# Second feed-forward matmul: six groups by seven products, low parts of the left operands on GpSimd

## The chip, the core and the metric

The kernel runs on one core of a Trainium2 chip. A core has TensorE (PE in the profile, with PEld for its weight loads), VectorE (DVE), ScalarE (ACT), GpSimd (POOL) and SyncE (SP, which issues the DMAs). Each has its own instruction stream, and they wait for each other by semaphores. The metric is the device time of one execution, in microseconds (us).

## What is computed

One layer of a streaming encoder: a modulated RMSNorm, a wide input projection, a gated branch and a matrix-memory branch, an output projection, and then the part that matters here, on 512 positions (`SEQ`) of width 1024:

```python
xn = modulate(rmsnorm(h, norm2_g[l]), sh2, sc2)
ff = jnp.square(jax.nn.relu(xn @ w_ff1[l])) @ w_ff2[l]
h = h + g2[:, None, :] * ff
```

and a final RMSNorm. `w_ff1` is 1024 x 4096 and `w_ff2` is 4096 x 1024, both in fp32.

## The kernel before

**Split operands.** Every fp32 operand of a matmul is split in two fp32r parts: a high part, rounded by a copy on ScalarE, and a low part, the operand minus the high part. A product is then three matmuls (`mm3`, lines 116 to 119): high by high, high by low, low by high. For the weights `w_pair` does this (ScalarE line 1082, VectorE line 1083; tiles `wh_g`/`wl_g` or `wh_x`/`wl_x`, 128 x 1024 elements). For the left operands, the activations, `hl` does it (ScalarE line 1099, VectorE line 1100; tiles `hsh`/`hsl`, 128 x 512 elements; the first two lie in `hs` tiles). The low parts for queries and keys early in the kernel are formed on GpSimd already (line 439), from operands of the same size as those of `hl`.

**Groups and products.** The second feed-forward matmul sums over 4096 rows of `w_ff2`. The first 3072 are taken in six groups of 512. In a group the activations form a 2 x 2 arrangement (`a11`, `a12`, `a21`, `a22`: two halves of the rows, two halves of the positions), and the weights too (`F11`, `F12`, `F21`, `F22`: two halves of the rows, two halves of the columns). A group marked "W" needs seven products of sums and differences of these (P1 to P7) instead of the plain eight. A group marked "S" takes the eight plainly, each added to the banks where it belongs (P2, P3, P4, E). Before, `GROUPS` is "WWWWWS". A "W" group needs in exchange: one difference of activations at the end of the first feed-forward matmul (`minus_a21`, line 1017), one of weights and three of activations in the first pass (lines 1115 and 1117 to 1119), and three of weights in the second pass (lines 1123, 1127, 1131), all on VectorE.

**Passes.** All groups are gone through twice. In the first pass a "W" group does P1, P2, P7, P3, in the second P5, P6, P4. `plan_` lists the steps, 43 of them, one per product and group. A step has 12 matmuls of 128 x 512 (two blocks of 128 positions, two blocks of 128 rows, three matmuls). Each product of the seven adds up over the groups in two PSUM banks of its own (`gP1` and so on). The banks are read on ScalarE or VectorE by `after` when a product's last step is past, and combined into `r` tiles.

**Order.** The loop over `plan_` asks for the operands of five steps ahead (`prefetch_step(5)`). Six high and six low tiles of activations (`hs_tile`) and five of weights are there, so a tile is written again when TensorE is done with a step before. A scheduler then orders each engine's stream. Weights come by DMAs from SyncE (`F` tiles, line 1060), seven in the air at most. Inside a group the differences of activations are made in place: lines 1117 to 1119 overwrite `a21`, `a12` and `a11` after `hl` has read them.

**Behind the passes.** The last 1024 rows of `w_ff2` are multiplied plainly, in pieces of 128 rows: four as they come (24 matmuls each), and four together at the end. Their banks are `ob`, for the first 256 positions, and, for the others, the two banks of P4 and the two of E, which go on with what the passes left there. The `r` tiles are meanwhile multiplied by the gate and added to the residual (`gated`, lines 1178 and 1179), and then the final norm follows.

Of the kernel before, what the change touches and what calls it, by code (L numbers as in the profile page):

```python
# [8 lines left out]
F32 = mybir.dt.float32  # L9
# [40 lines left out]
def block_kernel(ctx, tc, vecs_d, rows_d, ws_d, x_d, w_ada, w_in, w_out, w_ff1, w_ff2, out_d):  # L50
    nc = tc.nc
    act, dve, pool, pe, sp = nc.scalar, nc.vector, nc.gpsimd, nc.tensor, nc.sync
# [6 lines left out]
    def bank(nm):  # L59
        return psum.tile([P, 512], F32, tag="ps", name=nm)  # L60
# [55 lines left out]
    def mm3(out, ah, al, bh, bl, start, stop):  # L116
        pe.matmul(out, lhsT=ah, rhs=bh, start=start, stop=False)  # L117
        pe.matmul(out, lhsT=ah, rhs=bl, start=False, stop=False)  # L118
        pe.matmul(out, lhsT=al, rhs=bh, start=False, stop=stop)  # L119
# [488 lines left out]
    for i in range(TB):  # L608
        for j in range(i + 1):
            src = li[:, blk[i]] if j == i else frames[i][:, blk[j]]  # L610
# [114 lines left out]
    for half in range(2):  # L725
        cs = slice(half * 512, (half + 1) * 512)
# [7 lines left out]
    for half in range(2):  # L734
        cs = slice(half * 512, (half + 1) * 512)
# [23 lines left out]
    for half in range(2):  # L759
        cs = slice(half * 512, (half + 1) * 512)  # L760
# [6 lines left out]
        for k in range(4 * half, 4 * half + 4):  # L767
# [4 lines left out]
            h_, l_ = hl[:, 0], hl[:, 1]  # L772
# [237 lines left out]
        prefetch_op(2)  # L1010
        return bk.rearrange("p (f t) -> p f t", f=2)

    GROUPS = "WWWWWS"

    def minus_a21(n):
        if GROUPS[n:n + 1] == "W":
            dve.tensor_sub(out=hq[n, 0, 1], in0=hq[n, 0, 0], in1=hq[n, 0, 1])
# [21 lines left out]

    NF = len(GROUPS)  # L1040
    NK = FF // P
    KF = 4 * NF

    def later(kind, pas):
        return {("W", 0): ("P1", "P2", "P7", "P3"), ("W", 1): ("P5", "P6", "P4"),
                ("S", 0): ("P2", "P3", "P2", "P3"), ("S", 1): ("P4", "E", "P4", "E")}[kind, pas]
# [41 lines left out]
    def hs_tile(q):  # L1088
        return hsp.tile([P, 2, 256], F32R, tag="hs" + q, name=f"hs{q}{count[1]}", bufs=6)

    def hl(src):
        i = count[1]
        count[1] += 1
        if i < 2:
            both = fp.tile([P, 2, 2, 256], F32R, tag="sc", name=f"hs0{i}", bufs=2)
            h_, l_ = both[:, 0], both[:, 1]
        else:
            h_, l_ = hs_tile("h"), hs_tile("l")
        act.copy(out=h_, in_=src)  # L1099
        dve.tensor_sub(out=l_, in0=src, in1=h_.bitcast(F32))  # L1100
        return h_, l_

    def passes():
        for n in range(2):
            for nh in range(2):
                yield hl(hq[n, nh, 0]), w_pair(left.get(), left)
        for pas in range(2):
            for n, kind in enumerate(GROUPS):
                a11, a12, a21, a22 = hq[n, 0, 0], hq[n, 1, 0], hq[n, 0, 1], hq[n, 1, 1]
                if kind == "W" and pas == 0:  # L1110
                    if n > 1:
                        yield hl(a11), w_pair(left.get(), left)
                        yield hl(a12), w_pair(left.get(), left)
                    b12, b22 = right.get(), right.get()
                    dve.tensor_sub(out=b12, in0=b22, in1=b12)  # L1115
                    yield hl(a21), w_pair(b12, right)
                    dve.tensor_sub(out=a21, in0=a22, in1=a21)
                    dve.tensor_sub(out=a12, in0=a12, in1=a21)
                    dve.tensor_add(out=a11, in0=a21, in1=a11)
                    yield hl(a12), w_pair(b22, right)  # L1120
                elif kind == "W":
                    b11, b12 = left.get(), right.get()
                    dve.tensor_sub(out=b12, in0=b12, in1=b11)
                    left.more()
                    yield hl(a11), w_pair(b12)
                    b22 = right.get()
                    dve.tensor_sub(out=b22, in0=b22, in1=b12)  # L1127
                    right.more()
                    yield hl(a21), w_pair(b22)
                    b21 = left.get()  # L1130
                    dve.tensor_sub(out=b21, in0=b21, in1=b22)
                    right.more()
                    yield hl(a22), w_pair(b21, left)
                else:
                    for a_ in ((a11, a12), (a21, a22))[pas]:
                        x_ = hl(a_)
                        yield x_, w_pair(left.get(), left)
                        yield x_, w_pair(right.get(), right)

    plan_ = [(0, key) for key in ("P1", "P2") * 2 + ("P7", "P3") * 2]  # L1140
    plan_ += [(0, key) for kind in GROUPS[2:] for key in later(kind, 0)]
    plan_ += [(1, key) for kind in GROUPS for key in later(kind, 1)]
    gen = passes()
    ready = []

    def prefetch_step(m):
        while len(ready) < m:
            s_ = next(gen, None)
            if s_ is None:
                return  # L1150
            ready.append(s_)
# [13 lines left out]
    def hs_pair(kp):  # L1165
        for th in range(2):
            hsq[kp, th] = hl(hq[kp // 2, kp % 2, th])

    acc_b, res = {}, {}

    def rtile(nm, t):
        res[nm, t] = hsp.tile([P, 512], F32, name=f"r{nm}{t}")
        return res[nm, t]
# [7 lines left out]
    def after(key):  # L1181
        for t in range(2):
            b_ = acc_b.get((key, t))
            if key == "P1":
                act.copy(out=rtile("1", t), in_=b_)
            elif key == "P7":
                dve.tensor_add(out=rtile("7", t), in0=res["1", t], in1=b_)
            elif key == "P3":
                dve.tensor_add(out=rtile("3", t), in0=res["1", t], in1=b_)
            elif key == "P2":  # L1190
                dve.tensor_add(out=res["1", t], in0=res["1", t], in1=b_)
            elif key == "P6":
                dve.tensor_add(out=res["3", t], in0=res["3", t], in1=b_)
                dve.tensor_add(out=res["7", t], in0=res["7", t], in1=b_)
            elif key == "P5":
                dve.tensor_add(out=res["3", t], in0=res["3", t], in1=b_)
                dve.tensor_add(out=rtile("5", t), in0=res["7", t], in1=b_)

    last_of = {key: max(i for i, p_ in enumerate(plan_) if p_[1] == key) for _, key in plan_}
    end0 = max(i for i, p_ in enumerate(plan_) if p_[0] == 0)  # L1200
    jobs = {}
    for i_, keys in ((last_of["P7"] + 2, ("P1", "P7")), (end0 + 2, ("P3", "P2")),
                     (last_of["P4"] if GROUPS[-1] == "W" else last_of["P6"] + 3, ("P6", "P5"))):
        jobs.setdefault(i_, []).extend(keys)
    NS = len(plan_)
    for i, (pas, key) in enumerate(plan_):
        prefetch_step(5)
        (h_, l_), (wh, wl) = ready.pop(0)
        first = (key, 0) not in acc_b
        for t in range(2):  # L1210
            if first:
                acc_b[key, t] = bank(f"g{key}{t}")
            ts_ = slice(t * P, (t + 1) * P)
            for j in range(2):
                mm3(acc_b[key, t], h_[:, j, ts_], l_[:, j, ts_], wh[:, j], wl[:, j], first and j == 0,
                    i == last_of[key] and j == 1 and key not in ("P4", "E"))
        for key_ in jobs.get(i, ()):
            after(key_)
        if i == end0:
            sp.dma_start(out=fing, in_=rows_d[5].partition_broadcast(P))  # L1220
        if NS - i <= 4:
            ws_ff.prefetch(max(0, 4 - (NS - i)))
        if i == NS - 2:
            hs_pair(KF // 2)
# [1 line left out]
    ps_stack.close()  # L1226
    lwp = ff.enter_context(tc.tile_pool(name="lwp", bufs=1, side="right"))
    o_banks = [[bank(f"ob{t}{hf}") for hf in range(2)] for t in range(2)]
    o_banks += [[acc_b["P4", t], acc_b["E", t]] for t in range(2)]
    late = [(nm, t, row + t, hf) for nm, row, hf in (("1", 0, 0), ("3", 0, 1), ("7", 2, 0), ("5", 2, 1)) for t in range(2)]  # L1230

    def ff2_piece(k, last=False):
# [13 lines left out]
    def mm_f2(k, t, hf, wh, wl, stop):  # L1246
        cs = slice(hf * 512, (hf + 1) * 512)
        h_, l_ = (v[:, k % 2, (t % 2) * P:(t % 2 + 1) * P] for v in hsq[k // 2, t // 2])
        mm3(o_banks[t][hf], h_, l_, wh[:, 0, cs], wl[:, 0, cs], k == KF and t < 2, stop)

    for k in range(KF, NK - LAST):
        wh, wl = ff2_piece(k)
        for t in range(TB):
            for hf in range(2):
                mm_f2(k, t, hf, wh, wl, False)
        for _ in range(2):
            if late:
                gated(*late.pop(0))
# [46 lines left out]
    t = TB - 1  # L1305
# [72 lines left out]
```

## Time and profile before

| | us |
|---|---|
| median of 3 runs (806.1 to 807.3) | 807.0 |
| the profiled execution | 806.75 |
| its span in the trace | 805.0 |
| passes, first matmul to the first of the plain rows | 636.03 to 754.01 |

A row of instructions reads: start, duration, engine, line, operation, output and inputs by the program's names, and in brackets how long the engine was idle before and who ended that. A row of groups reads: count, total and mean duration in ns, and idle time before. The granted clock of TensorE is its share of full speed, 0.994 over the whole of this execution.

### The profile page before, as it was taken

What the parts mean: (1) busy time and instruction counts of PE and PEld (TensorE: products, weight loads), DVE (VectorE), ACT (ScalarE), POOL (GpSimd) and SP (SyncE); (2) the same over time, 40 slices, a digit from 0 to 9 for tenths busy, and PEclk for the clock granted to TensorE, in tenths of its full rate; (3) what the DMA queues carried; (4) which work ended last, traced back from release to release, by engine and by line L of the source; (5) the groups of instructions that cost most, each with busy time, mean ns of one, the idle gap of its engine ahead of it and who ended that gap; (6) DMA issues with size and microseconds to landing.
All of it is one profiled execution on the core that took longest, in us unless ns stands there. A gap on an engine that the chain in (4) does not pass through costs nothing.

```text
span 805.0 us, 11479 instructions
## 1 busy us (share of the span) xinstructions
PE 792.7 (98%) x4375; PEld 688.1 (85%) x4375; DVE 621.1 (77%) x938; ACT 404.2 (50%) x610; POOL 43.0 (5%) x62
## 2 busy tenths in 40 slices
PE   7999999999999999999999999999999999999996
PEld 6887888888988888888888899999999978888885
DVE  5889766774843348997847579888888799999966
ACT  5458566274533233242435247666666756646324
POOL 2004020121000000100000110000000000000000
PEclk8999999999999999999999999999999999999999
DMA  8974331143223388669337240333332466765302
GB/s 273 265 227 117 119 104 51 29 126 110 79 79 105 105 268 312 206 210 324 122 102 261 78 132 28 105 105 106 106 115 70 178 220 222 252 213 184 114 30 104
DMA packets 76423, 119.87 MB, mean 149 GB/s; under 512 B 5712, under 2 KB 38608, under 8 KB 76368
## 3 DMA queue, kind: packets, MB, share of 16 engines
q1 hardware_dynamic: 76368, 119.14, 46.6%
q8 instruction: 34, 0.56, 0.3%
q14 instruction: 21, 0.17, 0.1%
HBM read 117.02 MB, written 2.10 MB: 148 GB/s over the span
## 4 chain that ended last, share of the span: by engine, by line
PE 91%; DVE 2%; DMA 2%; ACT 2%; issue 1%; POOL 0%; SPq 0%; POOLq 0%; DVEq 0%
PE P L118 6%; PE P L117 6%; PE P L119 6%; PE gP L119 4%; PE gP L117 4%; PE gP L118 4%; PE qk L282 4%; PE wo L117 1%; PE wo L119 1%; PE wo L118 1%; PE cp L241 1%; PE k1b L117 1%; PE gb0b L118 1%; PE q1b L119 1%; PE gb0b L119 1%
## 5 line engine op out<-in xcount | busy, mean ns | idle before, releaser
L1099 ACT CAST hsh<-h 128x512 fp32r<-128x512 f32 x45 | 26.7, 620 | 26.9 <-PE gP L118 15.3
L1082 ACT CAST wh_g<-F 128x1024 fp32r<-128x1024 f32 x27 | 28.1, 1052 | 16.8 <-DVE F L1127 3.7
L119 PE MATMUL gP<-wh_g,hsl 128*128 128x512 f32 x92 | 35.8, 391 | 0.6 <-DVE hsl L1100 0.6
L118 PE MATMUL gP<-wl_g,hsh 128*128 128x512 f32 x92 | 35.8, 389 | 0.0
L117 PE MATMUL gP<-wh_g,hsh 128*128 128x512 f32 x92 | 35.7, 390 | 0.0
L1083 DVE TENSOR_TENSOR wl_g<-F,wh_g 128x1024 fp32r<-128x1024 f32 x27 | 32.9, 1225 | 0.8 <-ACT wh_g L1082 0.8
L921 ACT CAST wh_T<-T 128x1024 fp32r<-128x1024 f32 x21 | 22.0, 1048 | 20.0 <-PE P L118 18.4
L117 PE MATMUL P<-x2h,wh_B 128*128 128x256 f32 x112 | 31.6, 282 | 0.0
L118 PE MATMUL P<-x2l,wh_B 128*128 128x256 f32 x112 | 31.6, 282 | 0.0
L119 PE MATMUL P<-x2h,wl_B 128*128 128x256 f32 x112 | 31.6, 282 | 0.0
L921 ACT CAST wh_B<-B 128x1024 fp32r<-128x1024 f32 x21 | 22.0, 1049 | 16.4 <-PE P L118 15.4
L1100 DVE TENSOR_TENSOR hsl<-h,hsh 128x512 fp32r<-128x512 f32 x45 | 29.9, 692 | 0.3 <-ACT hsh L1099 0.3
L922 DVE TENSOR_TENSOR wl_T<-T,wh_T 128x1024 fp32r<-128x1024 f32 x21 | 25.7, 1224 | 3.0 <-ACT wh_T L921 2.9
L922 DVE TENSOR_TENSOR wl_B<-B,wh_B 128x1024 fp32r<-128x1024 f32 x21 | 25.6, 1220 | 0.0
L96 DVE TENSOR_TENSOR wl_gb<-raw_gb,wh_gb 128x1024 fp32r<-128x1024 f32 x8 | 9.8, 1224 | 19.7 <-ACT wh_gb L95 19.6
L118 PE MATMUL gP<-wl_x,hsh 128*128 128x512 f32 x64 | 24.9, 389 | 0.0
L117 PE MATMUL gP<-wh_x,hsh 128*128 128x512 f32 x64 | 24.9, 389 | 0.0
L119 PE MATMUL gP<-wh_x,hsl 128*128 128x512 f32 x64 | 24.9, 389 | 0.0
L667 DVE SCALAR_TENSOR_TENSOR accg<-arg,c_act,accg 128x1024 f32<-128x1024 f32 x14 | 18.0, 1283 | 6.5 <-DMA arg<-in_w_ada 6.3
L95 ACT CAST wh_ga<-raw_ga 128x1024 fp32r<-128x1024 f32 x8 | 8.4, 1052 | 27.2 <-PE ga0b L119 16.3
L976 ACT ACTIVATE h<-h 128x512 f32<-128x512 f32 x28 | 17.7, 632 | 8.5 <-DVE h L1036 4.0
L1082 ACT CAST wh_x<-F 128x1024 fp32r<-128x1024 f32 x16 | 16.6, 1050 | 9.5 <-DVE F L1115 3.9
(616 smaller groups left out, 2818.7 us busy)
## 6 DMA issues: line engine op xcount, KB each, us to landing
F<-in_w_ff SPq DMA_DIRECT2D x48, 512.0 KB, 4.2
B<-in_w_ff SPq DMA_DIRECT2D x28, 512.0 KB, 3.8
ar<-in_w_ada SPq DMA_DIRECT2D x64, 128.0 KB, 3.4
arg<-in_w_ada SPq DMA_DIRECT2D x16, 512.0 KB, 5.9
raw_f<-in_w_ff SPq DMA_DIRECT2D x12, 512.0 KB, 3.6
raw_o<-in_w_in SPq DMA_DIRECT2D x8, 512.0 KB, 4.1
raw_mv<-in_w_in SPq DMA_DIRECT2D x8, 512.0 KB, 3.6
raw_gb<-in_w_in SPq DMA_DIRECT2D x8, 512.0 KB, 3.7
```

Of the source, the lines that this page charges most:

```text
L117: pe.matmul(out, lhsT=ah, rhs=bh, start=start, stop=False)
L118: pe.matmul(out, lhsT=ah, rhs=bl, start=False, stop=False)
L119: pe.matmul(out, lhsT=al, rhs=bh, start=False, stop=stop)
L282: pe.matmul(bk, lhsT=wx[:, kk, f * P:(f + 1) * P], rhs=xx[k], start=k == 0 and ps_ == 0, stop=k == KT - 1 and ps_ == 2)
L667: dve.scalar_tensor_tensor(out=acc, in0=raw, scalar=c_act[:, k:k + 1], in1=acc, op0=ALU.mult, op1=ALU.add)
L921: act.copy(out=wh, in_=src)
L922: dve.tensor_sub(out=wl, in0=src, in1=wh.bitcast(F32))
L976: act.activation(dst, src, AF.Relu)
L1082: act.copy(out=wh, in_=src)
L1083: dve.tensor_sub(out=wl, in0=src, in1=wh.bitcast(F32))
L1099: act.copy(out=h_, in_=src)
L1100: dve.tensor_sub(out=l_, in0=src, in1=h_.bitcast(F32))
```

## The change

The last group becomes a "W" group as well, so that every group has seven products. The two banks of E are gone; the plain rows behind the passes get two fresh banks instead (`obr0`, `obr1`), so P6, which now goes to three results, is read into three `r` tiles, after P5 and at the end of the passes. And `hl` forms its low part on GpSimd instead of VectorE.

```diff
-    GROUPS = "WWWWWS"
+    GROUPS = "WWWWWW"
...
         act.copy(out=h_, in_=src)
-        dve.tensor_sub(out=l_, in0=src, in1=h_.bitcast(F32))
+        pool.tensor_sub(out=l_, in0=src, in1=h_.bitcast(F32))
...
-            elif key == "P6":
-                dve.tensor_add(out=res["3", t], in0=res["3", t], in1=b_)
-                dve.tensor_add(out=res["7", t], in0=res["7", t], in1=b_)
             elif key == "P5":
                 dve.tensor_add(out=res["3", t], in0=res["3", t], in1=b_)
                 dve.tensor_add(out=rtile("5", t), in0=res["7", t], in1=b_)
+            elif key == "P6":
+                for nm in ("3", "7", "5"):
+                    dve.tensor_add(out=res[nm, t], in0=res[nm, t], in1=b_)
...
-                     (last_of["P4"] if GROUPS[-1] == "W" else last_of["P6"] + 3, ("P6", "P5"))):
+                     (last_of["P5"] + 1, ("P5",)), (last_of["P6"] + 1, ("P6",))):
...
-    o_banks += [[acc_b["P4", t], acc_b["E", t]] for t in range(2)]
+    o_banks += [[acc_b["P4", t], bank(f"obr{t}")] for t in range(2)]
...
-        mm3(o_banks[t][hf], h_, l_, wh[:, 0, cs], wl[:, 0, cs], k == KF and t < 2, stop)
+        mm3(o_banks[t][hf], h_, l_, wh[:, 0, cs], wl[:, 0, cs], k == KF and (t < 2 or hf == 1), stop)
```

How this moves instructions shows at three places. On GpSimd, the stretch from the second norm (`rs2`) to the final one (`rs3`), which was empty; `h100` and its like are the activations, with the group as the first digit:

```order
 L76 TENSOR_TENSOR rs2_83<-rs2_83,mhalf_79 128x1
-L1284 TENSOR_TENSOR rs3_7460<-rs3_7460,mhalf_79 128x1 x4
+L1100 TENSOR_TENSOR hs00_6243<-h000_4528,hs00_6243 128x512
+L1100 TENSOR_TENSOR hs01_6252<-h010_4529,hs01_6252 128x512
+L1100 TENSOR_TENSOR hsl3_6279<-h100_4597,hsh3_6278 128x512
+L1100 TENSOR_TENSOR hsl4_6289<-h110_4599,hsh4_6288 128x512
+L1100 TENSOR_TENSOR hsl5_6300<-h001_4530,hsh5_6299 128x512
```

It now holds 50 such subtractions: 42 for the steps and 8 for the plain rows (before, VectorE had 39 and 8).

On VectorE, in the second pass at the fifth group (`F1243` is a weight tile of that group), before:

```order
L1123 TENSOR_TENSOR F1243_6944<-F1243_6944,F1143_6977 128x1024
L1100 TENSOR_TENSOR hsl35_7066<-h400_5311,hsh35_7065 128x512
L1127 TENSOR_TENSOR F2242_6967<-F2242_6967,F1243_6944 128x1024
L1083 TENSOR_TENSOR wl_g36_7070<-F1243_6944,wh_g36_7069 128x1024
L1100 TENSOR_TENSOR hsl36_7087<-h401_5312,hsh36_7086 128x512
L1083 TENSOR_TENSOR wl_g37_7091<-F2242_6967,wh_g37_7090 128x1024
L1131 TENSOR_TENSOR F2142_6992<-F2142_6992,F2242_6967 128x1024
L1100 TENSOR_TENSOR hsl37_7108<-h411_5314,hsh37_7107 128x512
```

and after, from the same difference on:

```order
L1123 TENSOR_TENSOR F1243_6957<-F1243_6957,F1143_6990 128x1024
L1083 TENSOR_TENSOR wl_x33_7012<-F1235_6866,wh_x33_7011 128x1024
L1127 TENSOR_TENSOR F2242_6980<-F2242_6980,F1243_6957 128x1024
L1083 TENSOR_TENSOR wl_x34_7035<-F2234_6899,wh_x34_7034 128x1024
L1131 TENSOR_TENSOR F2142_7005<-F2142_7005,F2242_6980 128x1024
L1178 TENSOR_TENSOR r10_6890<-r10_6890,rowg2_4096 128x512
L1083 TENSOR_TENSOR wl_g35_7058<-F2134_6932,wh_g35_7057 128x1024
L1123 TENSOR_TENSOR F1251_7028<-F1251_7028,F1151_7061 128x1024
L1083 TENSOR_TENSOR wl_g36_7083<-F1243_6957,wh_g36_7082 128x1024
```

The three subtractions of line 1100 have left VectorE's stream, and the differences of the sixth group (`F1251`) and a first instruction of `gated` have come in between the weight splits.

On VectorE, behind the last weight split of the passes, where P5 and P6 are read out of their banks, before:

```order
L1083 TENSOR_TENSOR wl_g42_7184<-F2250_7038,wh_g42_7183 128x1024
L1193 TENSOR_TENSOR r30_6912<-r30_6912,gP60_6898 128x512
L1194 TENSOR_TENSOR r70_6784<-r70_6784,gP60_6898 128x512
L1193 TENSOR_TENSOR r31_6914<-r31_6914,gP61_6905 128x512
L1194 TENSOR_TENSOR r71_6786<-r71_6786,gP61_6905 128x512
L1196 TENSOR_TENSOR r30_6912<-r30_6912,gP50_6871 128x512
```

and after (lines 1193 and 1194 are now the branch of P5, line 1197 that of P6):

```order
L1083 TENSOR_TENSOR wl_g41_7188<-F2150_7076,wh_g41_7187 128x1024
L96 TENSOR_TENSOR wl_f224_7230<-raw_f224_7227,wh_f224_7229 128x1024
L1193 TENSOR_TENSOR r30_6925<-r30_6925,gP50_6876 128x512
L1194 TENSOR_TENSOR r50_7246<-r70_6894,gP50_6876 128x512
L1193 TENSOR_TENSOR r31_6927<-r31_6927,gP51_6883 128x512
L1194 TENSOR_TENSOR r51_7249<-r71_6896,gP51_6883 128x512
L1197 TENSOR_TENSOR r30_6925<-r30_6925,gP60_6911 128x512
L1197 TENSOR_TENSOR r70_6894<-r70_6894,gP60_6911 128x512
L1197 TENSOR_TENSOR r50_7246<-r50_7246,gP60_6911 128x512
```

The split for the first plain rows (`wl_f224`) now stands ahead of these adds, and there are ten of them instead of eight.

More of the change, by code (lines that the diff above doesn't have):

```diff
@@ L1215, in block_kernel @@
                 mm3(acc_b[key, t], h_[:, j, ts_], l_[:, j, ts_], wh[:, j], wl[:, j], first and j == 0,
-                    i == last_of[key] and j == 1 and key not in ("P4", "E"))
+                    i == last_of[key] and j == 1 and key != "P4")
         for key_ in jobs.get(i, ()):
```

## The prediction

> **What bounds the kernel now.** I read the page first, then the busy time by stage, then who TensorE (PE) waits for in the last quarter, then single rows.
>
> ```profile
> PE 792.7 (98%) x4375; PEld 688.1 (85%) x4375; DVE 621.1 (77%) x938; ACT 404.2 (50%) x610; POOL 43.0 (5%) x62
> ...
> 640.00:750.00 110.00, 109.44 (x483) 90.11 (x482) 108.86 (x127) 63.44 (x83) 0.00 (x0) 1.00 0.66 216
> ...
> 754.00:805.00 51.00, 43.84 (x205) 36.61 (x203) 36.34 (x57) 18.46 (x34) 2.19 (x4) 0.97 0.23 83
> ...
> PE gP L119 <- DVE hsl L1100: 0.6, 1, 0.6
> ```
>
> In a row by stage the columns are the stretch, its length, then busy time of PE, PEld, DVE (VectorE), ACT (ScalarE) and POOL (GpSimd), granted clock, DMA share and GB/s. In the passes (640 to 750) PE is busy 109.44 of 110 us at a granted clock of 1.00, and VectorE 108.86. So two engines are full there. PE is the one that ends last, since from 600 us on it waited for another engine once, 0.6 us. GpSimd does nothing in the passes.
>
> ```profile
> 636.03 0.40 PE L117 MATMUL gP<-wh_g,hs 128*128 128x512 f32 x1
> ...
> 644.22 0.39 PE L117 MATMUL gP<-wh_x,hsh 128*128 128x512 f32 x1
> ...
> 649.66 0.39 PE L117 MATMUL gP<-wh_g,hsh 128*128 128x512 f32 x1
> ...
> 650.83 0.50 PE L119 MATMUL gP<-wh_g,hsl 128*128 128x512 f32 x1 [0.56 <-DVE hsl L1100]
> ...
> 754.01 0.39 PE L117 MATMUL ob<-wh_f,hsh 128*128 128x512 f32 x1
> ```
>
> The passes run from 636.03 to 754.01. Between 644.22 and 649.66 lie two steps of 12 matmuls, so a matmul takes 5.44/24 = 0.227 us and a step 2.72 us. The 0.39 of a row is a pipelined duration and no price. The single wait in brackets is for `hsl`, the instruction that the change moves.
>
> **PE's part of the change.** A "W" group has seven products and an "S" group eight, so 43 steps become 42: one step of 2.72 us less. If the 0.56 us wait goes too, PE alone would gain 3.3 us.
>
> **VectorE's own part.** I price VectorE by the distance of starts, not by row durations, which overlap.
>
> ```profile
> 642.00 1.23 DVE L1115 TENSOR_TENSOR F<-F,F 128x1024 f32<-128x1024 f32 x1 [0.54 <-DMA F<-in_w_ff]
> ...
> 665.25 1.23 DVE L1083 TENSOR_TENSOR wl_g<-F,wh_g 128x1024 fp32r<-128x1024 f32 x1
> 666.39 1.90 DVE L1100 TENSOR_TENSOR hsl<-h,hsh 128x512 fp32r<-128x512 f32 x3
> 668.20 1.23 DVE L1083 TENSOR_TENSOR wl_x<-F,wh_x 128x1024 fp32r<-128x1024 f32 x1
> 669.33 0.70 DVE L1100 TENSOR_TENSOR hsl<-h,hsh 128x512 fp32r<-128x512 f32 x1
> ...
> 743.28 0.69 DVE L1193 TENSOR_TENSOR r<-r,gP 128x512 f32<-128x512 f32 x1
> 743.87 0.69 DVE L1194 TENSOR_TENSOR r<-r,gP 128x512 f32<-128x512 f32 x1
> ...
> L1100 DVE TENSOR_TENSOR hsl<-h,hsh 128x512 fp32r<-128x512 f32 x45 | 29.9, 692 | 0.3 <-ACT hsh L1099 0.3
> L1100 DVE TENSOR_TENSOR hs<-h,hs 128x512 fp32r<-128x512 f32 x2 | 1.4, 688 | 0.7 <-ACT hs L1099 0.7
> ```
>
> A 1024-wide subtraction takes 1.135 us (665.25 to 666.39, 668.20 to 669.33), a 512-wide one 0.605 (three from 666.39 to 668.20), an add that reads PSUM 0.60 (743.28 to 743.87). The change takes 45 + 2 = 47 subtractions at 0.605 away, 28.4 us, and one weight split, 1.1. It adds the sixth group's four weight differences (4.5), its four activation differences (2.4; one of them in the first feed-forward matmul) and two PSUM adds (1.2). Net 21.4 us less, on an engine that is full. By this alone the change is harmless and a little good.
>
> **GpSimd's part decides.** It gets 50 subtractions of the kind that line 439 already runs there. What these do to VectorE is in the early rows:
>
> ```profile
> 66.35 7.96 DVE L433 SCALAR_TENSOR_TENSOR yb<-qk,vecs,yb 128x511 f32<-128x511 f32 x12
> ...
> 76.16 2.00 DVE L96 TENSOR_TENSOR wl_o<-raw_o,wh_o 128x1024 fp32r<-128x1024 f32 x1
> 78.08 2.31 DVE L96 TENSOR_TENSOR wl_k<-raw_k,wh_k 128x1024 fp32r<-128x1024 f32 x1
> ...
> 71.94 1.30 POOL L439 TENSOR_TENSOR q2l<-yb,q2h 128x512 fp32r<-128x512 f32 x1 [1.49 <-ACT q2h L438]
> 73.19 1.31 POOL L439 TENSOR_TENSOR q3l<-yb,q3h 128x512 fp32r<-128x512 f32 x1
> 75.79 1.29 POOL L439 TENSOR_TENSOR k0l<-yb,k0h 128x512 fp32r<-128x512 f32 x1 [1.29 <-ACT k0h L438]
> 77.64 1.67 POOL L439 TENSOR_TENSOR k1l<-yb,k1h 128x512 fp32r<-128x512 f32 x1 [0.56 <-ACT k1h L438]
> ...
> 114.18 1.23 DVE L96 TENSOR_TENSOR wl_mv<-raw_mv,wh_mv 128x1024 fp32r<-128x1024 f32 x1
> ...
> 114.74 1.81 POOL L439 TENSOR_TENSOR k4l<-cvk,k4h 128x512 fp32r<-128x512 f32 x1 [1.62 <-ACT k4h L438]
> ```
>
> Follow 75.79 to 80.39. `k0l` runs to 77.08. `wl_o`, begun at 76.16, ends at 78.16, which is 1.08 after `k0l`. `k1l`, begun at 77.64, ends at 79.31, 1.15 after `wl_o`. `wl_k`, begun at 78.08, ends at 80.39, again 1.08 after `k1l`. These run one after the other, although both engines had them issued. `wl_k` took 2.31 instead of about 1.22 us: the GpSimd instruction **cost VectorE 1.09 us**. At 114.18 VectorE was first and kept its 1.23, and GpSimd took 1.81 instead of 1.30. The twelve rows from 66.35, which read PSUM, took 0.66 each with `q2l` and `q3l` beside them, at 1.30: no conflict. All of VectorE's work in the passes except the PSUM adds is of the conflicting kind.
>
> On this the Trainium skill, SBUF — State Buffer, section "Who interferes with whom", has a rule: a VectorE instruction with two SBUF inputs and a GpSimd one that reads SBUF exclude each other, and the later one is blocked for the whole of the first. The trace agrees that they exclude each other, but the loss is 1.09 us and not the whole 1.30. By the whole 1.30 the sum below would be 835.5 instead of 828.
>
> **The sum.** VectorE's chain after the change starts at the same place, the first L1115 at 642.00, which waits for a DMA that the change doesn't touch. From there to the low part of the 39th step's weights its instructions are 59 of 1024 (67.0 us), 21 of 512 (12.7) and 6 PSUM adds (3.6): 83.3 us. GpSimd has done some five of its subtractions by 642 and runs about two steps ahead, so 36 fall in this stretch (steps 6 to 41): 36 x 1.09 = 39.2. The 39th weights are ready at 642.0 + 83.3 + 39.2 = 764.5. PE wants them at 636.03 + 456 x 0.227 = 739.4. VectorE is then the bound, 25 us late. Its last three splits follow closely, so PE's last four steps run at PE's rate: the passes end at 764.5 + 4 x 2.72 - 0.23 = 775.2, against 754.0 before: **+21.2 us**. I stop at the 39th step since a later one gives an earlier end.
>
> The rest I cost at nothing. After the passes a piece has 24 matmuls (5.44 us) against VectorE's one split and four 512-wide instructions (3.6 us) and at most two GpSimd subtractions in two pieces; 6.6 of 8.1 us that VectorE waits there lie before its first output row:
>
> ```profile
> DVE ot L1271 <- PE ob L119: 8.1, 4, 6.6
> ...
> L1099 ACT CAST hsh<-h 128x512 fp32r<-128x512 f32 x45 | 26.7, 620 | 26.9 <-PE gP L118 15.3
> ```
>
> The P6 adds come later than before, but the fresh bank `obr0` is first written 15 matmuls (3.4 us) after the passes' end and its three adds can start a step (2.72) before it; if that cover is gone it costs up to their 1.8 us. The two subtractions that fall into the first feed-forward matmul cost VectorE 2.2 us where it has idle time. ScalarE, at 63.44 of 110 us, has room for three more casts of 0.62.
>
> The profiled execution took 806.75 us (span 805.0), beside a median of 807.0: 806.75 + 21.2 = **828 us**.
>
> **Bounds of the unknown.** What a GpSimd subtraction costs a VectorE that always has another instruction queued is shown once (1.09). From below: 34 instead of 36 of them, and all six PSUM adds beside them, gives 822; a tenth of the collisions less, 818. From above: the whole 1.30 each, 835.5. Below zero it can't go, since a removed instruction is counted already. I take 1.09, the row with the same shapes on both engines.
>
> **Rivals.**
> - *No price: PE stays the bound, and it is faster.* VectorE without loans would be ready at 725.3 and PE wants step 39 at 739.4: 14.1 us of slack over 36 instructions. If one costs VectorE under 0.39 us, GpSimd's work is hidden and only PE's saving is left: 806.75 - 2.72 - 0.56 = 803.5. For it speaks that the changed VectorE has 21.4 us less to do; against it the four ends above, which fit to 0.02 us. Chance 0.09.
> - *Half a price.* Where GpSimd's instructions find VectorE at PSUM adds or waiting, they cost less. At 0.55 us each the passes end at 755.8, at 0.8 at 764.8: 808.5 to 817.5. Against it: VectorE has almost no idle time to be found in. Chance 0.10, of which 0.02 within 0.2% of no change (which is about what a measurement of this kernel can tell apart).
> - *Waits on top.* L1117 and L1118 overwrite activations that GpSimd must first have read. VectorE then stands still in its queue, with every following split behind it. If each of the six groups waits for one cast (0.62) and one subtraction (1.30), it is 11.5 us more: 839. Against it: GpSimd's rows stand two to three steps ahead. Chance 0.10.
>
> My forecast, 818 to 836, has 0.71. The range 813 to 840 adds half of each neighbour, some 0.81. Faster 0.09, same 0.02, slower 0.89.
>
> **What will show it.** If I am right: L1083 and L1115 to L1131 take some 1.6 to 2.3 us on average instead of 1.22, L1100 on GpSimd 1.3 to 2.3; PE shows many waits, most of them for `wl_g` and `wl_x` of VectorE, growing from the second group on and larger in the second pass; the passes end near 775, and from there to the end it is again 51 us. If PE is still full in the passes and L1083 keeps 1.22 us, the first rival holds. If VectorE shows idle time before L1117, released by GpSimd, it is the third. A lower granted clock in the passes, or a longer tail, would be something that I haven't counted.

## The result, and the profile after

The changed kernel takes a median of 831.3 us (831.1 to 832.3, 4 runs) beside 806.6 us (804.8 to 807.3, 4 runs) before: a ratio of 1.0313, with a 95% interval of 1.0294 to 1.0332. It is slower by 3.1%, where 828 us (813 to 840) was forecast. The profiled execution took 831.19 us, of which 829.4 are its span.

First the busy times of the page, then the stretches of the passes, of the stall in the middle of them and of the work behind them (columns as before: PE, PEld, DVE, ACT, POOL, granted clock, DMA share, GB/s), and all that TensorE waited for from 600 us on (total, times, longest):

```profile
PE 797.0 (96%) x4363; PEld 685.9 (83%) x4363; DVE 639.0 (77%) x900; ACT 403.8 (49%) x612; POOL 140.2 (17%) x112
...
640.00:750.00 110.00, 93.19 (x386) 72.36 (x386) 102.50 (x75) 52.53 (x71) 69.14 (x36) 0.97 0.57 188
...
720.00:730.00 10.00, 7.09 (x23) 5.75 (x24) 10.00 (x12) 2.62 (x3) 4.69 (x3) 0.66 0.58 184
...
778.00:829.00 51.00, 44.02 (x206) 36.77 (x204) 37.91 (x56) 18.36 (x34) 11.98 (x7) 0.97 0.24 84
...
PE gP L118 <- DVE wl_g L1083: 7.1, 7, 1.5
PE gP L117 <- DVE r L1187: 6.7, 1, 6.7
PE gP L118 <- DVE wl_x L1083: 5.8, 6, 1.8
PE gP L119 <- POOL hsl L1100: 0.5, 2, 0.2
```

TensorE, which was busy 109.44 of the 110 us from 640 to 750, is now busy 93.19 of them. In the passes it waited once before; now it waits for VectorE fourteen times, 19.6 us together. VectorE executes 75 instructions in these 110 us instead of 127 and is still busy 102.50 us. The first matmul of the plain rows starts at 778.19 instead of 754.01. So the passes end 24.2 us later, and from there to the end of the span it is 51.2 us, as before (51.0): the whole loss lies in the passes.

What made VectorE slow shows in its groups between 640 and 770 us (count, busy, mean in ns, idle time before and whom it waited for), with GpSimd's group behind them:

```profile
L1083 DVE TENSOR_TENSOR wl_g<-F,wh_g 128x1024 fp32r<-128x1024 f32 x22 | 36.4, 1661 | 0.0
L1083 DVE TENSOR_TENSOR wl_x<-F,wh_x 128x1024 fp32r<-128x1024 f32 x16 | 25.6, 1602 | 1.8 <-ACT wh_x L1082 1.8
L1123 DVE TENSOR_TENSOR F<-F,F 128x1024 f32<-128x1024 f32 x6 | 12.8, 2137 | 1.1 <-DMA F<-in_w_ff 1.1
L1115 DVE TENSOR_TENSOR F<-F,F 128x1024 f32<-128x1024 f32 x6 | 11.7, 1946 | 1.3 <-DMA F<-in_w_ff 1.3
L1131 DVE TENSOR_TENSOR F<-F,F 128x1024 f32<-128x1024 f32 x6 | 10.5, 1753 | 0.0
L1127 DVE TENSOR_TENSOR F<-F,F 128x1024 f32<-128x1024 f32 x6 | 9.5, 1576 | 0.0
L1119 DVE TENSOR_TENSOR h<-h,h 128x512 f32<-128x512 f32 x6 | 6.3, 1050 | 0.0
...
L1117 DVE TENSOR_TENSOR h<-h,h 128x512 f32<-128x512 f32 x6 | 4.1, 684 | 4.9 <-POOL hsl L1100 4.9
L1178 DVE TENSOR_TENSOR r<-r,rowg 128x512 f32<-128x512 f32 x2 | 2.5, 1232 | 0.0
L1179 DVE TENSOR_TENSOR yb<-yb,r 128x512 f32<-128x512 f32 x2 | 2.5, 1228 | 0.0
...
L1189 DVE TENSOR_TENSOR r<-r,gP 128x512 f32<-128x512 f32 x2 | 1.3, 674 | 0.0
...
L1100 POOL TENSOR_TENSOR hsl<-h,hsh 128x512 fp32r<-128x512 f32 x41 | 78.2, 1930 | 51.4 <-ACT hsh L1099 51.4
```

A subtraction of 128 x 1024 that took 1.22 us before takes 1.58 to 2.14 on average, while the adds that read PSUM (L1189) keep their 0.67. Added up over the groups, count times the mean above 1.22 (or 0.69), VectorE's rows are 35.3 us longer than alone; 41 subtractions of GpSimd ran beside them, **0.86 us for each**. GpSimd's own take 1.93 instead of 1.30.

Row by row, where both engines are full (start, duration; the GpSimd row is eight subtractions in a piece):

```profile
713.31 2.31 DVE L1127 TENSOR_TENSOR F<-F,F 128x1024 f32<-128x1024 f32 x1
715.55 2.31 DVE L1083 TENSOR_TENSOR wl_g<-F,wh_g 128x1024 fp32r<-128x1024 f32 x1
717.77 2.28 DVE L1131 TENSOR_TENSOR F<-F,F 128x1024 f32<-128x1024 f32 x1
719.98 2.28 DVE L1083 TENSOR_TENSOR wl_g<-F,wh_g 128x1024 fp32r<-128x1024 f32 x1
722.18 1.27 DVE L1187 TENSOR_TENSOR r<-r,gP 128x512 f32<-128x512 f32 x2
723.38 1.21 DVE L1123 TENSOR_TENSOR F<-F,F 128x1024 f32<-128x1024 f32 x1
...
706.72 16.67 POOL L1100 TENSOR_TENSOR hsl<-h,hsh 128x512 fp32r<-128x512 f32 x8 [7.62 <-ACT hsh L1099]
```

The two engines take turns. While GpSimd's piece runs (to 723.39), every VectorE subtraction that begins in it takes about 2.3 us, 1.09 more than alone; the two L1187, which read PSUM, aren't delayed, and with the end of the piece the next subtraction is back at 1.21.

### The profile page after: what moved, and what is told of

Read it like the earlier page. It is cut to its first block, busy times and chain, and to the rows that moved or that the text cites. A ratio compares the mean times of both kernels' runs of the same rounds, so it can differ in the third digit from the quotient of the medians.

```text
span 829.4 us, 11538 instructions
## 1 busy us (share of the span) xinstructions
PE 797.0 (96%) x4363; PEld 685.9 (83%) x4363; DVE 639.0 (77%) x900; ACT 403.8 (49%) x612; POOL 140.2 (17%) x112
## 4 chain that ended last, share of the span: by engine, by line
PE 81%; DVE 11%; issue 3%; DMA 2%; ACT 1%; POOL 1%; SPq 0%; POOLq 0%; DVEq 0%; ACTq 0%
PE P L119 6%; PE P L117 6%; PE P L118 6%; PE qk L282 4%; DVE wl_g L1083 3%; PE wo L117 2%; PE wo L119 2%; PE wo L118 2%; DVE wl_x L1083 1%; DVE F L1123 1%; PE cp L241 1%; DVE F L1131 1%; PE gP L118 1%; PE f10b L118 1%; PE f10b L119 1%
## 5 line engine op out<-in xcount | busy, mean ns | idle before, releaser
L1100 POOL TENSOR_TENSOR hsl<-h,hsh 128x512 fp32r<-128x512 f32 x48 | 94.5, 1989 | 73.3 <-ACT hsh L1099 73.3
L1099 ACT CAST hsh<-h 128x512 fp32r<-128x512 f32 x48 | 28.7, 618 | 40.5 <-DVE h L1118 24.2
L118 PE MATMUL gP<-wl_g,hsh 128*128 128x512 f32 x96 | 39.1, 408 | 7.4 <-DVE wl_g L1083 7.1
L117 PE MATMUL gP<-wh_g,hsh 128*128 128x512 f32 x96 | 38.3, 399 | 6.7 <-DVE r L1187 6.7
L1083 DVE TENSOR_TENSOR wl_g<-F,wh_g 128x1024 fp32r<-128x1024 f32 x26 | 42.3, 1635 | 0.5 <-ACT wh_g L1082 0.5
L119 PE MATMUL gP<-wh_g,hsl 128*128 128x512 f32 x96 | 38.3, 399 | 0.5 <-POOL hsl L1100 0.5
L118 PEld LDWEIGHTS gP<-wl_g,hsh 128*128 128x128 f32 x96 | 18.4, 192 | 14.8 <-DVE wl_g L1083 11.2
L117 PEld LDWEIGHTS gP<-wh_g,hsh 128*128 128x128 f32 x96 | 18.6, 193 | 11.0 <-DVE r L1187 7.1
L1100 POOL TENSOR_TENSOR hs<-h,hs 128x512 fp32r<-128x512 f32 x2 | 2.6, 1299 | 146.2 <-ACT hs L1099 146.2
L1083 DVE TENSOR_TENSOR wl_x<-F,wh_x 128x1024 fp32r<-128x1024 f32 x16 | 25.6, 1602 | 1.8 <-ACT wh_x L1082 1.8
L75 POOL TENSOR_SCALAR rs<-ss 128x1 f32<-128x1 f32 x4 | 2.3, 568 | 142.1 <-ACT sc L836 142.1
```

What stands on the lines that cost most here:

```text
L1083: dve.tensor_sub(out=wl, in0=src, in1=wh.bitcast(F32))
L1100: pool.tensor_sub(out=l_, in0=src, in1=h_.bitcast(F32))
```

## The experiments

**Theory.** VectorE is the bound, and each GpSimd subtraction takes it about 1 us. **Rivals.** The seven products themselves cost the time; VectorE stands in its queue for GpSimd (L1117); the 6.7 us that TensorE waits for L1187 are a loss of their own. Ratios are to the kernel before, with 95% intervals.

**1. The products alone.** All six groups by seven products, low parts on VectorE (edit of the changed kernel):

```diff
-        pool.tensor_sub(out=l_, in0=src, in1=h_.bitcast(F32))
+        dve.tensor_sub(out=l_, in0=src, in1=h_.bitcast(F32))
```

> The change without GpSimd: six groups of seven products, low parts on VectorE as before. My theory (VectorE's stream decides, GpSimd's instructions take turns with it): VectorE's own sum is then 17 us longer than in the changed kernel, but nothing is taken from it; by distances of starts it has the 39th weights ready at 742.4 where TensorE wants them at 739.6, so the passes end at some 753.3 instead of 754.0 and the time is 804.5 to 807.5, with VectorE full and TensorE waiting some 2 to 4 us. Rival (TensorE alone decides, the loss of the change is in the seven products or in their read-out): for the first half of it 803.5, with no waits; for the second, still above 820.

Measured: 804.6 us, ratio 0.9983 (0.9970 to 0.9997); the passes end at 751.45, 2.56 us earlier than before. Its stretch:

```profile
640.00:750.00 110.00, 109.15 (x474) 87.88 (x473) 109.88 (x127) 64.05 (x84) 0.00 (x0) 1.00 0.64 207
```

The products bring about the step of 2.72 us that they save, and no loss: the second half of the rival falls. TensorE waited 0.8 us in all, where my theory wanted 2 to 4, and VectorE, busy 109.88 of 110 us, had the 39th weights ready at 740.5 and not at 742.4. So the two engines are level here, and this run doesn't show which of them decides. Experiment 5, with the same useful work, takes the same time; no version of the study is clearly faster.

**2. GpSimd alone.** The kernel before with `GROUPS = "WWWWWS"`, only line 1100 changed:

```diff
-        dve.tensor_sub(out=l_, in0=src, in1=h_.bitcast(F32))
+        pool.tensor_sub(out=l_, in0=src, in1=h_.bitcast(F32))
```

> The kernel before with the low parts of the left operands on GpSimd, and nothing else. My theory: VectorE's own sum to the 39th weights ends at 719.5, and 35 subtractions of GpSimd take 0.96 to 1.09 us each from it: 753 to 758 and the passes end at 767 to 771, with the stalls of the changed kernel (7 us) at 774: 820 to 828. Rival (the loss comes from the products and their read-out): 806 to 808.

Measured: 830.1 us, ratio 1.0298 (1.0276 to 1.0321), a little above the expected band; the passes end at 773.61. The move to GpSimd alone costs as much as the whole change. Summed as above from 640 us to the end of the passes, VectorE's rows lost 31.0 us to 40 GpSimd subtractions, and VectorE stood idle 13.5 us, more than I had counted: 6.0 before L1117, 5.2 for DMAs and 2.3 for ScalarE.

**3. GpSimd work whose result nobody uses.** The kernel of experiment 1, and GpSimd forms a difference that isn't used, once per low part of the passes and plain rows (`idle_t` is a tile of 128 x 512):

```diff
         dve.tensor_sub(out=l_, in0=src, in1=h_.bitcast(F32))
+        if i >= 2:
+            pool.tensor_sub(out=idle_t, in0=h_.bitcast(F32), in1=h_.bitcast(F32))
```

> The run without GpSimd (e1), with a subtraction on GpSimd added beside each low part, 128 x 512, both inputs the high part, its output never used. Nobody waits for its result. My theory: some 36 to 40 of them are taken from a VectorE that has no slack, about 1 us each: e1 plus 32 to 42 us, 837 to 848. Rival (the loss is the later arrival of the low parts, not the turns): e1, 804 to 808, since nothing arrives later; at most a few us from the later release of the high parts.

Measured: 842.3 us, ratio 1.0445 (1.0425 to 1.0464). VectorE has the instructions of experiment 1, and no engine reads GpSimd's result, yet the time is 38 us longer. Not all of that is the turns, as TensorE's longest waits and GpSimd's rows show (in the last row the shortest, median and longest, in ns):

```profile
PE gP L117 <- ACT wh_g L1082: 12.2, 4, 7.1
...
649.41 20.71 POOL L1102 TENSOR_TENSOR idle_t<-hsh 128x512 f32<-128x512 f32 x3 [8.23 <-ACT hsh L1099]
...
L1102 POOL TENSOR_TENSOR idle_t<-hsh x48: 1039/1368/18150, 637.2 to 816.8; 128x512 f32<-128x512 f32 x48
```

From 640 us to the end of the passes (788.1) VectorE's rows are 28.3 us longer than alone, with 43 of these subtractions beside them: 0.66 us for each. (The shortest took 1.04 us, not 1.30; both of its inputs are the same tile.) The rest came by waits. GpSimd reads the high part, so ScalarE can't write that tile again before GpSimd is done, and the first subtraction of the piece at 649.41 took 18.2 us. ScalarE waited 14.9 us for such reads, TensorE 20.2 us for ScalarE, and VectorE stood idle 7.5 us, nearly all of it for ScalarE. With the 28.3 us these 7.5 make 35.8 of the 36.6 us by which the passes end later than in experiment 1. So the rival of the expectation, the later release of the high parts, is a part of the loss and more than the few us that I gave it; the turns are the larger part.

**4. The same with a single input.**

```diff
-            pool.tensor_sub(out=idle_t, in0=h_.bitcast(F32), in1=h_.bitcast(F32))
+            pool.tensor_copy(out=idle_t, in_=h_.bitcast(F32))
```

> The six groups with all low parts on VectorE, and a GpSimd copy (one input, 128 x 512) of every high part of the passes, whose output nobody uses. Theory (any GpSimd instruction that reads SBUF shuts a two-input VectorE instruction out for as long as it reads): with a copy of 0.5 to 1.0 us, 36 to 40 in the passes cost 18 to 38 us, 820 to 842. Rival (the price comes from GpSimd's second input): 804 to 808, as with the memsets.

Measured: 825.1 us, ratio 1.0221 (1.0197 to 1.0244). VectorE's largest group between 640 and 770 us:

```profile
L1083 DVE TENSOR_TENSOR wl_g<-F,wh_g 128x1024 fp32r<-128x1024 f32 x23 | 30.0, 1305 | 2.5 <-ACT wh_g L1082 2.5
```

A single input is enough. Where the two engines take turns, a row takes 1.63 instead of 1.22 us, 0.41 more, beside a copy that takes 0.61 alone. But up to the end of the passes (771.8) VectorE's rows lost only 11.9 us to 44 copies, 0.27 for each, less than the 18 us at the foot of my band. VectorE was also idle for 7.3 us, most of it waiting for ScalarE as in experiment 3 (the longest copy took 17.7 us). That the time fell into the band is in part luck.

**5. GpSimd work that only writes.** Two memsets of the same tile in place of the subtraction:

```diff
-            pool.tensor_sub(out=idle_t, in0=h_.bitcast(F32), in1=h_.bitcast(F32))
+            pool.memset(idle_t, 0.0)
+            pool.memset(idle_t, 1.0)
```

> The same as the run with idle subtractions, with two memsets of 128 x 512 (about 1 us together) in place of each subtraction: GpSimd is as busy but reads nothing. My theory (only instructions that read two inputs from SBUF take turns with those of GpSimd that read SBUF): as e1 within 1 us. Rival (any work of GpSimd holds VectorE up, or its instruction stream does): plus 20 us or more.

Measured: 805.0 us, ratio 0.9986 (0.9975 to 0.9997), as without them. The memsets wait for nothing and ran in a piece from 634 to 690 us; a stretch of it (first row) and VectorE's group from 634 to 690:

```profile
640.00:690.00 50.00, 49.55 (x218) 40.57 (x218) 50.00 (x61) 29.53 (x38) 45.11 (x86) 1.00 0.70 229
...
L1083 DVE TENSOR_TENSOR wl_g<-F,wh_g 128x1024 fp32r<-128x1024 f32 x13 | 15.9, 1221 | 0.3 <-ACT wh_g L1082 0.3
```

GpSimd is busy 45.11 of 50 us and VectorE's subtractions stay at 1221 ns. So it isn't that GpSimd is busy, but that it reads. The memsets also hold no tile that ScalarE wants to write, so the times of experiments 3 and 5 alone don't part the turns from the waits; the lengths of VectorE's rows do.

**6. Half of it.** The changed kernel, every second low part back on VectorE:

```diff
-        pool.tensor_sub(out=l_, in0=src, in1=h_.bitcast(F32))
+        (pool if i % 2 else dve).tensor_sub(out=l_, in0=src, in1=h_.bitcast(F32))
```

> The changed kernel, but only every second low part of the left operands is formed by GpSimd, the others by VectorE as before. Theory (a price per GpSimd subtraction on a full VectorE): half of the thefts (some 18 x 1.0 us in the passes), 18 own subtractions of 0.605 us put back, and somewhat less idle time before L1117, so the passes end at 764 to 769 and the time is 816 to 823. Rival 1 (the loss is mainly VectorE's standing still for GpSimd in its queue before L1117, not the price): most of the loss stays, over 826. Rival 2 (a threshold, with slack that hides a part): under 810.

Measured: 829.1 us, ratio 1.0277 (1.0258 to 1.0296): above my theory's band, and the number of the first rival. Its reason isn't there, though: VectorE waited for GpSimd once in the passes, 2.4 us before L1118. Half of the GpSimd work costs nearly as much as all of it. The GpSimd rows, VectorE beside them, and what TensorE waited for in the passes:

```profile
722.77 23.07 POOL L1100 TENSOR_TENSOR hsl<-h,hsh 128x512 fp32r<-128x512 f32 x3 [10.90 <-ACT hsh L1099]
...
738.17 1.21 DVE L1123 TENSOR_TENSOR F<-F,F 128x1024 f32<-128x1024 f32 x1
739.30 1.21 DVE L1083 TENSOR_TENSOR wl_g<-F,wh_g 128x1024 fp32r<-128x1024 f32 x1
740.44 0.68 DVE L1100 TENSOR_TENSOR hsl<-h,hsh 128x512 fp32r<-128x512 f32 x1
741.04 1.21 DVE L1127 TENSOR_TENSOR F<-F,F 128x1024 f32<-128x1024 f32 x1
749.33 1.47 DVE L1083 TENSOR_TENSOR wl_g<-F,wh_g 128x1024 fp32r<-128x1024 f32 x1 [7.08 <-ACT wh_g L1082]
...
PE gP L119 <- POOL hsl L1100: 14.5, 3, 7.1
PE gP L117 <- DVE r L1187: 4.9, 1, 4.9
...
L1100 POOL TENSOR_TENSOR hsl<-h,hsh x24: 1267/1739/20606, 638.2 to 786.9; 128x512 fp32r<-128x512 f32 x24
```

Here the first GpSimd subtraction of the piece at 722.77 takes 20.6 us (the largest of its line, in the last row: min, median, max). Beside it VectorE runs eighteen instructions at their undisturbed 1.21 and 0.68, and GpSimd gets through only when VectorE stops at 742.25. TensorE waits 7.1 us for that low part, and 1.6 and 5.7 for two others. VectorE's rows lost half as much as in the changed kernel (some 15 us between 640 and 770, summed as above, for 20 subtractions), as the theory wants; what was gained there was lost to **GpSimd instructions that did not get their turn**.

**7 and 8. Is it the idle time?** Most of the subtractions shut out so had followed 7 us or more of idle GpSimd. So I kept it from idling. Experiment 7 is experiment 6 with a small memset on each low tile that VectorE fills:

```diff
+        if i % 2 == 0 and i >= 2:
+            pool.memset(l_[:, 0, 0:64].bitcast(F32), 0.0)
         (pool if i % 2 else dve).tensor_sub(out=l_, in0=src, in1=h_.bitcast(F32))
```

> Every second low part on GpSimd, as in the run before it, and for the low parts that VectorE forms a GpSimd memset of 128 x 64 on the tile first, so that GpSimd is never idle for long. In the run without it, the GpSimd subtractions that came after some 8 us or more of idle GpSimd were shut out while VectorE ran 2 to 18 instructions back to back, 20.6 us in the worst case, and TensorE waited for them. Theory (an idle GpSimd loses its turn, and that made up what the halving should have saved): GpSimd's instructions of over 3 us vanish, TensorE's waits for hsl too, only the price of some 20 subtractions is left: 814 to 822. Rival (the idle time has nothing to do with it): instructions of 7 to 20 us are still there, and the time is 826 to 831.

Experiment 8 is a case apart from it, a kernel in which GpSimd forms only the eight low parts of the plain rows (experiment 1 with `pool` for those of `hs_pair`):

```diff
-    def hl(src):
+    def hl(src, eng=dve):
...
+        eng.tensor_sub(out=l_, in0=src, in1=h_.bitcast(F32))
...
-            hsq[kp, th] = hl(hq[kp // 2, kp % 2, th])
+            hsq[kp, th] = hl(hq[kp // 2, kp % 2, th], pool)
```

> The six groups of seven products with all low parts of the passes on VectorE; GpSimd forms only the eight low parts for the plain rows behind the passes. Theory (a GpSimd subtraction costs VectorE time, but there VectorE isn't the bound): no change against the products alone, 803.5 to 806. Rival (the price counts wherever GpSimd works): 8 x 1.0 us more, 810 to 813.

This was run as it stands, and then with such memsets in the passes:

```diff
+        if eng is dve and i >= 2:
+            pool.memset(l_[:, 0, 0:64].bitcast(F32), 0.0)
         act.copy(out=h_, in_=src)
```

> GpSimd forms only the eight low parts behind the passes, as in the run before it, and during the passes it writes a memset of 128 x 64 into each low tile before VectorE fills it. In the run without it the first GpSimd subtraction, after 260 us of idle time, took 12.1 us beside VectorE's instructions. Theory (an idle GpSimd loses its turn): no GpSimd subtraction over 3 us, each takes VectorE about 1 us instead, and the time is 803 to 808. Rival (idle time has nothing to do with it): a first subtraction of some 10 us again, and the same 808 to 810.

Measured: the half with memsets 823.0 us, ratio 1.0210 (1.0191 to 1.0228), just above the theory's band, with one row of 8.0 us left in the passes, as the rival wanted; the plain rows alone 808.8 us, 1.0031 (1.0017 to 1.0045), between the two expectations (where the 4 us beyond experiment 1 come from is not shown); with memsets 809.1 us, 1.0046 (1.0029 to 1.0063), the rival's. The low parts of the plain rows on GpSimd, first without memsets, then with (min, median, max in ns):

```profile
L1100 POOL TENSOR_TENSOR hsl<-h,hsh x8: 1291/1778/12142, 739.3 to 764.3; 128x512 fp32r<-128x512 f32 x8
```

```profile
735.32 0.15 POOL L1100 MEMSET hsl<- 128x64 f32 x1 [2.34 <-PE gP L119]
739.03 13.40 POOL L1102 TENSOR_TENSOR hsl<-h,hsh 128x512 fp32r<-128x512 f32 x2 [3.56 <-ACT hsh L1101]
...
L1102 POOL TENSOR_TENSOR hsl<-h,hsh x8: 1297/1788/12147, 739.0 to 764.0; 128x512 fp32r<-128x512 f32 x8
```

The same subtraction is shut out for the same 12.1 us after 3.56 us of idle time as after 260. **My theory of the idle time falls.** The memsets read nothing, so they don't test the time since GpSimd's last read. Against that speaks the changed kernel: its piece at 706.72 came after 7.62 us without a read, and its eight subtractions took 2.1 us each, while one of 8.1 us in experiment 2 came after 4.14. That the half gained 6 us by the memsets goes with fewer long rows (8.0 us at most in the passes, not 20.6), but the memsets also changed when things start, and VectorE waited 8.9 us for them; what decides whether GpSimd gets its turn stays open. Against chance speaks that the lengths repeat at the same place of the program (12.14 and 12.15 us here, 18.15 and 17.73 for the first long one of experiments 3 and 4).

**9 and 10. Is the wait for L1187 a loss of its own?** First I asked for the reads of P1 and P7 two steps earlier:

```diff
-    for i_, keys in ((last_of["P7"] + 2, ("P1", "P7")), (end0 + 2, ("P3", "P2")),
+    for i_, keys in ((last_of["P7"], ("P1", "P7")), (end0 + 2, ("P3", "P2")),
```

> The changed kernel with one edit: the banks of P1 and P7 are read out two steps earlier in the program's order, so that TensorE need not stand 6.7 us before P5's first matmul for L1187. Theory (VectorE's sum sets the end of the passes, and the wait is only where the lateness shows): same time, 829 to 833, and the wait shows before weight splits instead. Rival (the wait, and the lower granted clock behind it, are a loss of their own on top of VectorE's sum): 822 to 826.

Measured: 830.1 us, ratio 1.0291 (1.0273 to 1.0309). It says nothing: the scheduler left L1187 in its place in VectorE's stream, and the wait was 6.7 us again. Then I had ScalarE empty the banks:

```diff
             elif key == "P7":
-                dve.tensor_add(out=rtile("7", t), in0=res["1", t], in1=b_)
+                act.copy(out=rtile("7", t), in_=b_)
+                dve.tensor_add(out=res["7", t], in0=res["7", t], in1=res["1", t])
```

> The changed kernel, with P7's two banks read by copies on ScalarE, and VectorE adding the copies later, so that TensorE need not wait for VectorE before P5's first matmul; VectorE has as many instructions as before. (The run with the earlier place for the reads moved only ScalarE's copy of P1; VectorE's L1187 stayed in its row and the wait of 6.7 us too, so that it tells nothing of this wait.) Theory (VectorE's sum sets the end of the passes; the wait is only where its lateness shows): the 6.7 us wait goes or shrinks, waits for weights take its place, same time, 828 to 833. Rival (the wait, and the lower clock behind it, are a loss of their own): 822 to 826.

Measured: 832.1 us, ratio 1.0326 (1.0302 to 1.0350). TensorE's waits:

```profile
PE gP L117 <- DVE r L1190: 7.9, 1, 7.9
PE gP L118 <- DVE wl_g L1083: 6.5, 6, 1.5
PE gP L118 <- DVE wl_x L1083: 4.4, 5, 1.8
```

The wait for L1187 is gone, TensorE waits 7.9 us for the next bank instead, which VectorE reads on L1190, and the time stays. So this run moves the wait and doesn't remove it, and can't tell by itself what the wait costs. The trace of the changed kernel can: from the L1123 at 708.79 to the end of the passes VectorE's instructions follow each other without a wait. TensorE's stall, from 716 to 723, held up none of them, and the end of the passes follows from VectorE's last weights, as the next section adds up. So the wait is no loss on top of VectorE's lateness.

## Why the prediction was right

**The bound.** That VectorE would take TensorE's place, at some price per GpSimd subtraction, is shown: by the turns row by row, by experiment 2 (the move alone makes the loss), and by experiments 3 and 5 (GpSimd work whose result nobody uses makes VectorE's rows 28.3 us longer if it reads, and no longer if it only writes).

**The sum to the 39th step.** Its weights were forecast for 764.5 and came here:

```profile
641.76 2.30 DVE L1115 TENSOR_TENSOR F<-F,F 128x1024 f32<-128x1024 f32 x1
...
651.72 0.69 DVE L1117 TENSOR_TENSOR h<-h,h 128x512 f32<-128x512 f32 x1 [2.44 <-POOL hsl L1100]
...
663.94 0.69 DVE L1117 TENSOR_TENSOR h<-h,h 128x512 f32<-128x512 f32 x1 [2.44 <-POOL hsl L1100]
...
766.03 1.21 DVE L1083 TENSOR_TENSOR wl_x<-F,wh_x 128x1024 fp32r<-128x1024 f32 x1
```

From 641.76 to 767.24 it is 125.5 us, where 122.5 was forecast. VectorE's own 83.3 us held. The term of 39.2 us (36 subtractions at 1.09) measured 33.8: the 35.3 of the groups less what two rows outside this stretch lost. More of them fell into it, some 39, at 0.86 each, since those that meet a PSUM add or a standing VectorE take nothing. And 7.3 us of idle time were not in the sum: 4.9 at L1117 and 2.4 for DMAs (1.1 us of the 125.5 remain unplaced). So a term that was 5.4 too large and one of 7.3 that was missing nearly cancelled: the mechanism was right, but that the sum came so close is luck. The forecast's last step, four steps of TensorE behind these weights, fits: 767.24 + 10.65 = 777.9, measured 778.19.

**The rivals.** "No price" falls with 0.86 us for each; the point from which it decides was 0.39. (Of the distances between ends by which I argued against it, the two of 1.08 us agree; the third, 1.15, has no second to compare.) "Half a price" ended at 0.8, so it falls by little, and its reason, GpSimd meeting PSUM adds or a standing VectorE, goes some of the way from 1.09 to 0.86. "Waits on top" was no rival but a part: two of the six groups wait, 2.44 us each, where I had priced six at 1.92.

**The rule of the Trainium skill** (SBUF — State Buffer, sections "Who interferes with whom" and "SBUF: two separate sides") that a VectorE instruction with two SBUF inputs and a GpSimd one that reads SBUF exclude each other: the runs agree, and experiment 5 agrees with its other half, that a GpSimd instruction that only writes doesn't contend. That the later one is blocked for the whole of the first is near, not exact: 1.09 us where the two take turns, of a subtraction that takes 1.30 alone. And GpSimd can be blocked for much more than one instruction, 20.6 us in experiment 6.

**TensorE's side.** The saved step is in experiment 1 (2.56 of 2.72 us). That the tail would stay as it was held too. The wait for L1187 I had not foreseen, only waits for weights; it is the same lateness of VectorE in another place.

## What to carry to other kernels

Before work goes to an idle engine, ask what it shares with the engine that is full. Here 47 subtractions of 0.6 us taken from VectorE cost 24 us, since GpSimd's reads shut VectorE's two-input subtractions out for longer than those had taken VectorE itself, and since engines then waited for GpSimd; work for GpSimd beside a full VectorE is work that only writes, or that meets VectorE at PSUM operands. And a price that is found in rows of another stage of the same kernel (four ends between 75 and 81 us) carried: 1.09 us where both engines were full, 0.86 on average.

## What was not expected of the hardware

**A GpSimd instruction can be shut out for long.** In most rows the two engines take turns at each instruction. In a few a waiting GpSimd subtraction sees VectorE run on undelayed, for 6.2 us behind the passes of the changed kernel, 8.1 in experiment 2, 20.6 in experiment 6, and is let in, in all those of 12 us and more, only when VectorE pauses or reads PSUM. Idle time before it doesn't explain it. That the lengths repeat points to the sequence of instructions; what in the sequence, no run shows.

**TensorE's clock behind a stall.** After the wait for L1187 the matmuls come 0.43 us apart for some 3.4 us, then 0.23 again, and the granted clock from 720 to 730 us was 0.66:

```profile
722.91 0.80 PE L117 MATMUL gP<-wh_g,hsh 128*128 128x512 f32 x1 [6.68 <-DVE r L1187]
723.50 0.63 PE L118 MATMUL gP<-wl_g,hsh 128*128 128x512 f32 x1
723.93 0.63 PE L119 MATMUL gP<-wh_g,hsl 128*128 128x512 f32 x1
...
726.86 0.40 PE L117 MATMUL gP<-wh_g,hsh 128*128 128x512 f32 x1
727.10 0.39 PE L118 MATMUL gP<-wl_g,hsh 128*128 128x512 f32 x1
```

This agrees with the Trainium skill, TensorE: Matmul & The Clock Gate, part 1, by which the array falls to half its clock after an idle window of about 3.4 us and needs as much busy time to come back. After the wait of 7.1 us in experiment 6 the slow matmuls went on for 4.9 us. Eight matmuls at 0.2 us more are 1.6 us; as VectorE was the bound, they weren't missed.
